# Shift and scale of the first norm: from four column quarters on VectorE to two column halves on TensorE

## The chip, the cores and the metric

The kernel runs on one core of a Trainium2 chip. The metric is device time in microseconds (us) of one execution. The engines are TensorE (PE in the profile; its weight loads are PEld), VectorE (DVE), ScalarE (ACT), GpSimd (POOL) and SyncE (SP), which here does nothing but start transfers from HBM.

## What is computed

One layer of a hybrid streaming encoder on 256 tokens of width 1024: a normalised and modulated input, a projection into two groups of heads, an output projection, and then a mixture of 32 experts, each token going to four. The change touches only the first line of the modulation:

```
c_act = silu(c)
mod = c_act @ w_ada + b_ada                      # 1024 x 6144 weights
sh1, sc1, g1, sh2, sc2, g2 = split(mod, 6)
h = rms_norm(x, pre_mix_norm) * (1.0 + sc1) + sh1
proj = h @ w_in                                  # 1024 x 2216 weights
```

The first 2048 columns of `w_ada` (8 MB in float32) give `sh1` and `sc1`. The expert weights, 384 MB, are read in full.

## The kernel before

All weights pass through a ring of seven buffers of 1 MB (`Stream`, L72, `RING` = 7). `want` lists a load, `take` gives the buffer to its user, and `done` frees it, whereupon `pump` issues the next load of the list on the SP queue. Two more buffers, `x0` and `x1`, belong to the experts; nothing uses them earlier, so the loads of two `gu` tiles into them may be issued at any time. The program is written in a logical order, and a planner that simulates the engines' times fixes the order of the instructions on each engine (`issue_after` and `keep_in_program_order` only bind it). Engines then run their own list strictly in that order.

Opening stage. `x` is normalised, scaled and transposed into `hT`, eight blocks (`k`) of 128 columns of x by 256 tokens. The matmul of the projection needs each block multiplied by `a1` = (1 + sc1) * gain and shifted by `sh1`; it is formed twice, as a rounded part `hTh` (ScalarE, L468) and a remainder `hTl` (VectorE, L470 and L471). The blocks are used in four steps `q` of two blocks each:

- `mod_sum(q)` (L444) takes two buffers `mod` holding all 1024 rows of a quarter of the columns, 256 of the shift and 256 of the scale, and adds eight products row block by row block on VectorE (L451, L453) into `md`. One row of a transfer is a contiguous run of 256 columns, 1 KB.
- `mod_use(q)` (L457) sums `md` over the partitions with four small matmuls against ones into `mc` (L459; the trace counts each as two records), adds the bias (`half`, L463), forms `a1` (L465), and then `hTh` and `hTl` of two blocks.
- `split_xbc(q)` and `split_nat(q)` cut a buffer of `w_in` into a rounded part `whi` on ScalarE (L424) and a remainder `wlo` (L427), on VectorE for xbc, on GpSimd for nat.
- `in_xbc(q)` (L483) is 48 matmuls of 256 columns into the four banks `pa`; `in_nat(q)` (L497) is 24 matmuls into the banks `pn0`, `pn1` and `pn2`. Of each three (L432, L433, L434) one needs `wlo` and one `hTl`.

After the last `in_nat` the banks `pn` are copied out (L532, L533), `gate_in` (L559) projects `z` into the banks `pz`, with its remainders on GpSimd (L563), and a long stage of attention, state-space mixing and routing follows. From about 215 us on the experts run: `up` (L1191) multiplies by `gu` tiles and `down` by `dn` tiles, all loaded through the ring.

PSUM has eight banks: four of tag A (`pa`), two of tag B (`pn0`, `pn1`) and two of tag Z, handed out in turn. Z goes to `mc`, `pn2`, then `pz0` and `pz1`: `pz0` follows `mc` and `pz1` follows `pn2`. Later (L633) the same kernel forms other columns of `mod` on TensorE: `ada` multiplies a row block by `crep`, 32 equal columns of silu(c), into four groups of 32 PSUM rows (L642).

Of the kernel before, what the change touches and what calls it, by code (L numbers as in the profile page):

```python
# [15 lines left out]
OP = mybir.AluOpType  # L16
# [4 lines left out]
S = 256  # L21
P = 128
TT = S // P
KT = D // P
# [42 lines left out]
E_C, E_PM, E_B1, E_END = 0, 8, 16, 32  # L67
# [39 lines left out]
def body(ctx, tc, a, out, ne=NE):  # L107
    nc = tc.nc
    V, A, G, T, SP = nc.vector, nc.scalar, nc.gpsimd, nc.tensor, nc.sync
# [24 lines left out]
    v1, v2, v3 = (tl([P, 2048], f"v{i}", f"v{i}") for i in (1, 2, 3))  # L134
# [32 lines left out]

    st_ = Stream(sb, [f"w{j}" for j in range(RING)])
    w_ada = a["w_ada"].rearrange("l (k p) c -> p (l k) c", p=P)
    w_adq = a["w_ada"].rearrange("l (k p) (s q c) -> p (l k) s q c", p=P, q=4, c=256)  # L170
    w_in = a["w_in"].rearrange("l (k p) c -> p (l k) c", p=P)
    w_q = a["w_q_up"].rearrange("l (k p) c -> p (l k) c", p=P)
    w_kv = a["w_kv_up"].rearrange("l (k p) c -> p (l k) c", p=P)
# [5 lines left out]
    def ld(view, src):  # L179
        def f(t):  # L180
            SP.dma_start(view(t), src)

        return f

    def want_mod(q):
        for k0 in (0, 4):

            def f(t, k0=k0):
                tv = t.rearrange("p (k s c) -> p k s c", k=4, s=2)
                for s in range(2):  # L190
                    SP.dma_start(tv[:, :, s, :], w_adq[:, k0 : k0 + 4, s, q, :])

            st_.want(f"mod{q}{k0}", f)

    def halves(t):
        return t.rearrange("p (k c) -> p k c", k=2)
# [1 line left out]
    def natv(t):  # L198
        return t[:, :1360].rearrange("p (k c) -> p k c", k=2)
# [7 lines left out]
    def ld_nat(k0):  # L207


        def f(t):  # L210
            tv = natv(t)
            SP.dma_start(tv[:, :, 0:392], w_in[:, k0 : k0 + 2, 1536:1928])
            SP.dma_start(tv[:, :, 392:424], w_in[:, k0 : k0 + 2, 2184:2216])
            SP.dma_start(tv[:, :, 424:680], w_in[:, k0 : k0 + 2, 1928:2184])

        return f

    def some(n):
        for _ in range(min(n, len(small))):
            dst, src = small.pop(0)  # L220

            def f(dst=dst, src=src):
                tc.keep_in_program_order(SP.dma_start(dst, src))

            st_.side(f)

    want_mod(0)
    for q in range(4):
        st_.want(f"xbc{2 * q}", ld(halves, w_in[:, 2 * q : 2 * q + 2, 512:1536]))
        if q < 3:  # L230
            want_mod(q + 1)
        st_.want(f"nat{2 * q}", ld_nat(2 * q))
    some(8)
    for k0 in range(0, KT, 4):
        st_.want(f"z{k0}", ld(zv, w_in[:, k0 : k0 + 4, 0:512]))
# [62 lines left out]
    ones = tl([P, P], "ones")  # L298
# [30 lines left out]
    with ExitStack() as fc:  # L329
# [106 lines left out]


        a1 = tl([P, KT], "a1")
        mc = bank("mc", "Z")

        sums = {}
        last_mod = [None]

        def mod_sum(q):  # L444
            ac = two([P, 512], "md")
            for k0 in (0, 4):
                w = st_.take(f"mod{q}{k0}").rearrange("p (k n) -> p k n", k=4)
                for k in range(4):
                    c = cact[:, k0 + k : k0 + k + 1]
                    if k0 + k == 0:  # L450
                        V.tensor_scalar(ac, w[:, k, :], c, None, op0=OP.mult)  # L451
                    else:
                        V.scalar_tensor_tensor(ac, w[:, k, :], c, ac, op0=OP.mult, op1=OP.add)  # L453
                st_.done(f"mod{q}{k0}")
            sums[q] = ac

        def mod_use(q):  # L457
            for j in range(4):
                T.matmul(mc[:, 4 * q + j : 4 * q + j + 1], sums[q][:, j * P : (j + 1) * P], ones[:, 0:1], start=q + j == 0, stop=True,  # L459
                         skip_group_check=True)  # L460
            half = two([P, 2, 2], "mh")
            ksl = slice(2 * q, 2 * q + 2)
            V.tensor_tensor(half, mc[:, 4 * q : 4 * q + 4].rearrange("p (s k) -> p s k", s=2),  # L463
                            prE[:, E_B1 : E_B1 + 16].rearrange("p (s k) -> p s k", s=2)[:, :, ksl], op=OP.add)
            V.scalar_tensor_tensor(a1[:, ksl], half[:, 1, :], 1.0, prE[:, E_PM + 2 * q : E_PM + 2 * q + 2], op0=OP.add, op1=OP.mult)  # L465
            for j in range(2):
                k = 2 * q + j
                A.activation(hTh[:, k, :], hT[:, k, :], AF.Identity, bias=half[:, 0, j : j + 1], scale=a1[:, k : k + 1])  # L468
                tm = v2[:, 1024 + S * j : 1024 + S * j + S]
                V.tensor_scalar(tm, hT[:, k, :], a1[:, k : k + 1], half[:, 0, j : j + 1], op0=OP.mult, op1=OP.add)  # L470
                last_mod[0] = V.tensor_tensor(hTl[:, k, :], tm, hTh[:, k, :], op=OP.subtract)  # L471

# [5 lines left out]
        def split_xbc(q):  # L478
            w = [halves(v) for v in split(st_.take(f"xbc{2 * q}"), wh[q % 2], wl[q % 2], parts=2)]
            st_.done(f"xbc{2 * q}")  # L480
            return w

        def in_xbc(q, w):  # L483
            k0 = 2 * q
            for k in (0, 1):
                for ct in range(8):
                    mm3(pa[ct // 2][:, ct % 2, :], [v[:, k, ct * P : (ct + 1) * P] for v in w], (hTh[:, k0 + k, :], hTl[:, k0 + k, :]),
                        k0 + k == 0 and ct % 2 == 0, k0 + k == KT - 1, skip_group_check=True)

        pn = []  # L490

        def split_nat(q):
            w = [natv(v) for v in split(st_.take(f"nat{2 * q}"), "f7", "f8", 1360, eng=G)]
            st_.done(f"nat{2 * q}")
            return w

        def in_nat(q, w):  # L497
            k0 = 2 * q
            for k in (0, 1):
                for t in range(TT):  # L500
                    h = [v[:, k0 + k, t * P : (t + 1) * P] for v in (hTh, hTl)]
                    mm3(pn[t][:, :424], h, [v[:, k, 0:424] for v in w], k0 + k == 0, k0 + k == KT - 1)
                    mm3(pn[2][:, t * 256 : t * 256 + 256], h, [v[:, k, 424:680] for v in w], k0 + k + t == 0, k0 + k == KT - 1,
                        skip_group_check=True)

        mod_sum(0)
        mod_use(0)
        pa += [bank(f"pa{j}").rearrange("p (c s) -> p c s", c=2) for j in range(4)]
        pn += [bank("pn0", "B"), bank("pn1", "B"), bank("pn2", "Z")]
        for q in range(4):  # L510
            if q == 0:
                with tc.issue_after(last_mod[0].ins):
                    wx = split_xbc(q)
            else:
                wx = split_xbc(q)
            if q < 3:
                mod_sum(q + 1)
            wn = split_nat(q)
            in_xbc(q, wx)
            if q < 3:  # L520
                mod_use(q + 1)
            in_nat(q, wn)


# [896 lines left out]
    for e in range(ne):  # L1421
# [43 lines left out]
        ac = act(e, gs, 2 if e == last else 1)  # L1465
# [40 lines left out]
    for i, tag in ((0, "gu"), (1, "pc"), (2, "tp")):  # L1506
        c0, w = parts[i]
# [65 lines left out]
```

## Time and profile before

| | us |
|---|---|
| median of three runs | 1167.58 |
| lowest and highest | 1167.48, 1169.38 |
| the profiled execution | 1165.31 |
| its span, first to last instruction | 1163.5 |
| TensorE busy in the span | 1064.9 |
| VectorE busy | 446.1 |

The profile is of one execution. A row of its timeline gives the start of a group of equal instructions, its duration, the engine, the line, what is written from what, the number of instructions, and in brackets the idle time of that engine just before and what ended it. Consecutive matmuls overlap, so the step from one start to the next is the price of one in a stream, and its duration is the latency of one. A table by stretches gives the busy time of each engine, the granted clock of TensorE (1.00 is 2.4 GHz, 0.50 is 1.2 GHz), the busy share of the transfer engines and their rate in GB/s. Some 449 MB are moved.

### The profile page before, as it was taken

How to read it: one execution, taken by the hardware profiler on the slowest of the kernel's cores; microseconds unless marked ns; L12 is line 12 of the kernel's file. 1: busy time of each engine (PE TensorE's matmuls, PEld its weight loads, DVE VectorE, ACT ScalarE, POOL GpSimd, SP SyncE). 2: the span in 40 equal slices, each digit the busy share in tenths (PEclk: the TensorE clock that was granted, in tenths of full speed). 3: DMA queues.
4: the chain of work that ended last, by engine and by line, in shares of the span. 5: the costliest groups of instructions: out<-in, count | busy, mean ns of one | idle time of the engine just before them, and what ended most of it. 6: DMA issues, size and time to landing. Idle time of an engine off the chain costs nothing. (4 is left out here: it accounts for less than half of the span.)

```text
span 1163.5 us, 13379 instructions
## 1 busy us (share of the span) xinstructions
PE 1064.9 (92%) x5078; PEld 452.4 (39%) x5078; DVE 446.1 (38%) x921; ACT 190.5 (16%) x364; POOL 68.1 (6%) x68
## 2 busy tenths in 40 slices
PE   4899998989999999998989899989898998989996
PEld 4885774333333333332323233323233232333332
DVE  6869855333332323232323232332314142323224
ACT  5365443100111100100101000100101010101003
POOL 1254430000000000000000000000000000000000
PEclk9899999999999999999999899999999898999998
DMA  9987799879989999999999999999999999999992
GB/s 337 324 328 314 262 376 361 343 290 368 412 358 422 420 406 420 421 422 420 421 420 422 420 421 420 420 421 422 419 422 422 421 422 420 421 415 420 422 356 88
DMA packets 79915, 449.23 MB, mean 386 GB/s; under 512 B 10385, under 2 KB 23166, under 8 KB 29090
## 3 DMA queue, kind: packets, MB, share of 16 engines
q1 hardware_dynamic: 79362, 447.43, 94.5%
q8 instruction: 74, 1.21, 0.4%
q14 instruction: 63, 0.52, 0.1%
q10 hardware_dynamic: 416, 0.07, 0.0%
HBM read 446.42 MB, written 1.05 MB: 385 GB/s over the span
## 5 line engine op out<-in xcount | busy, mean ns | idle before, releaser
L1195 PE MATMUL gu<-gu,xT 128*64 128x512 f32 x2048 | 475.3, 612 | 35.6 <-DMA gu<-in_w_gate_up 33.8
L1195 PEld LDWEIGHTS gu<-gu,xT 128*64 128x64 f32 x2048 | 145.5, 140 | 317.7 <-issue 262.4
L1243 PE MATMUL py<-dn,ac 128*64 128x512 f32 x992 | 220.6, 597 | 0.2 <-DVE ac L1231 0.2
L1243 PEld LDWEIGHTS py<-dn,ac 128*64 128x64 f32 x992 | 70.8, 138 | 144.6 <-issue 126.2
L1252 DVE COPY cm<-py 64x512 f32<-64x512 f32 x30 | 20.8, 695 | 212.9 <-ACT cm L1251 212.9
L1201 DVE COPY gs<-gu 128x512 f32<-128x512 f32 x31 | 21.4, 691 | 174.9 <-PE gu L1195 174.9
L1281 PE MATMUL pc<-cm,gtm 128*128 128x512 f32 x120 | 60.8, 635 | 11.5 <-DVEq L1360 10.1
L1200 ACT COPY gs<-gu 128x512 f32<-128x512 f32 x32 | 18.7, 585 | 314.0 <-PE gu L1195 314.0
L1174 PE MATMUL pg<-x,oh 128*64 128x512 f32 x256 | 60.6, 594 | 2.9 <-DVEq L1360 2.2
L1282 DVE TENSOR_TENSOR acc<-acc,pc 128x512 f32<-128x512 f32 x64 | 44.0, 687 | 39.7 <-PE pc L1281 39.6
L1536 POOL TENSOR_TENSOR x<-x,acc 128x512 f32<-128x512 f32 x1 | 1.3, 1262 | 923.8 <-ACT acc L1535 923.8
L1184 DVE TENSOR_TENSOR xT<-pgt,md 128x512 f32<-128x512 f32 x32 | 22.1, 691 | 82.8 <-PE pgt L1182 82.8
L1222 DVE TENSOR_TENSOR u<-tp,biasT 128x512 f32<-128x512 f32 x64 | 41.5, 685 | 29.4 <-PE tp L1215 29.1
L1251 ACT COPY cm<-py 64x512 f32<-64x512 f32 x30 | 17.4, 579 | 191.3 <-PE py L1243 191.3
L1170 DVE TENSOR_SCALAR oh<-cst,rkp,r 128x64 f32<-128x64 f32 x64 | 17.2, 311 | 82.0 <-PE pg L1174 82.0
L1215 PEld LDWEIGHTS tp<-ident,gs 128*128 128x128 f32 x256 | 34.6, 206 | 27.9 <-ACTq L1360 16.4
L1215 PE MATMUL tp<-ident,gs 128*128 128x128 f32 x256 | 38.0, 289 | 6.6 <-PEq L1360 5.3
L1281 PEld LDWEIGHTS pc<-cm,gtm 128*128 128x128 f32 x120 | 19.9, 193 | 52.0 <-DVEq L1360 19.8
L1176 ACT COPY xg<-pg 128x512 f32<-128x512 f32 x32 | 18.7, 585 | 127.2 <-PE pg L1174 127.2
L1228 ACT ACTIVATE sg<-u 128x512 f32<-128x512 f32 (+1 forms) x33 | 20.4, 618 | 95.5 <-DVE u L1227 91.9
L1174 PEld LDWEIGHTS pg<-x,oh 128*64 128x64 f32 x256 | 18.0, 137 | 39.4 <-issue 38.6
L1259 DVE TENSOR_SCALAR go<-cst,rkp,gate 128x64 f32<-128x64 f32 x128 | 30.0, 308 | 0.6 <-DVEq L1360 0.6
(403 smaller groups left out, 956.4 us busy)
## 6 DMA issues: line engine op xcount, KB each, us to landing
gu<-in_w_gate_up SPq DMA_DIRECT2D x256, 1024.0 KB
dn<-in_w_down SPq DMA_DIRECT2D x124, 1024.0 KB
ada<-in_w_ada SPq DMA_DIRECT2D x16, 1024.0 KB
mod<-in_w_ada SPq DMA_DIRECT2D x16, 512.0 KB
xbc<-in_w_in SPq DMA_DIRECT2D x4, 1024.0 KB
wo<-in_w_out SPq DMA_DIRECT2D x4, 1024.0 KB
z<-in_w_in SPq DMA_DIRECT2D x2, 1024.0 KB
dn<-in_w_down SPq DMA_DIRECT2D x4, 512.0 KB
```

The source lines that it names most:

```text
L1174: T.matmul(pg[64 * h : 64 * h + 64, :], oh[:, t, :], x[:, t, h * 512 : h * 512 + 512], start=t == 0, stop=t == TT - 1)
L1184: V.tensor_tensor(xT.rearrange("p (h q) s -> p q h s", h=2), pg, a2.rearrange("p (h q) -> p q h", h=2)[:, :, :, None].to_broadcast([P, 4, ...
L1195: T.matmul(gu[h][64 * g : 64 * g + 64, :], xT[:, k, :], ws[k][:, g * 1024 + h * 512 : g * 1024 + h * 512 + 512], start=k == 0, stop=k == K ...
L1201: copy(gs[1], gu[1])
L1215: T.transpose(tp[f // 4][:, f % 4].rearrange("p g s -> p (g s)"), gs[f // 4][:, rows_of(f % 4)], ident)
L1222: V.tensor_tensor(u[:, hs], tp[h], bv[:, hs, :, None].to_broadcast([P, 4, 2, CAP]), op=OP.add)
L1228: A.activation(sg[:, fs], u[:, fs, 0, :], AF.Sigmoid, scale=1.702)
L1243: T.matmul(py[64 * g : 64 * g + 64, :], ac[:, f, :], wd(f, ch), start=f == 0, stop=f == FT - 1)
L1252: V.tensor_copy(comb[(e & 1) ^ 1][64:128, :], py[64:128, :])
L1259: V.tensor_scalar(go[:, t, j, :], iota, rkp[:, t, ee : ee + 1], gate[:, t, ee : ee + 1], op0=OP.is_equal, op1=OP.mult)
L1281: T.matmul(pc, lhs(t, ch), rhs(ch), start=bias is None or (t, ch) != bias_left[0], stop=True)
L1282: V.tensor_tensor(acc[:, t, ch * 512 : ch * 512 + 512], acc[:, t, ch * 512 : ch * 512 + 512], pc, op=OP.add)
```

## The change

The columns are taken in two halves instead of four quarters, and the sum over the rows is done by TensorE. A buffer `mod` now holds two row blocks of half the columns (512 of the shift, 512 of the scale; runs of 2 KB), so a half takes four buffers. `mod_sum(h)` multiplies each row block by `crep`, in 16 matmuls that write four groups of 32 rows of one bank `mo` (row blocks even and odd, shift and scale), and copies the bank to `md` on ScalarE. `mod_use(h)` sums the groups with four small matmuls against a two-column selector `sel` into `mc`, which now lies in unused columns of the bank of `pn0`, and forms four blocks of `hTh` and `hTl`. The first half stands ahead of everything; the second is placed in step `q` = 1, between `in_xbc(1)` and `in_nat(1)`. The list of loads changes accordingly.

```
-    want_mod(0)
+    want_mod(0, (0, 2, 4, 6))
     for q in range(4):
         st_.want(f"xbc{2 * q}", ld(halves, w_in[:, 2 * q : 2 * q + 2, 512:1536]))
-        if q < 3:
-            want_mod(q + 1)
+        if q < 2:
+            want_mod(1, (4 * q,))
         st_.want(f"nat{2 * q}", ld_nat(2 * q))
+        if q < 2:
+            want_mod(1, (4 * q + 2,))
...
-        mc = bank("mc", "Z")
+        sel = tl([P, 2], "sel")
+        V.memset(sel, 0.0)
+        for g in range(4):
+            V.memset(sel[32 * g : 32 * g + 1, g % 2 : g % 2 + 1], 1.0)
+        pn = [bank("pn0", "B")]
+        mc = pn[0][:, 440:456]
...
-        def mod_sum(q):
-            ac = two([P, 512], "md")
-            for k0 in (0, 4):
-                w = st_.take(f"mod{q}{k0}").rearrange("p (k n) -> p k n", k=4)
-                for k in range(4):
-                    c = cact[:, k0 + k : k0 + k + 1]
-                    if k0 + k == 0:
-                        V.tensor_scalar(ac, w[:, k, :], c, None, op0=OP.mult)
-                    else:
-                        V.scalar_tensor_tensor(ac, w[:, k, :], c, ac, op0=OP.mult, op1=OP.add)
-                st_.done(f"mod{q}{k0}")
-            sums[q] = ac
+        def mod_sum(h):
+            b = bank("mo", "Z")
+            for k0 in range(0, KT, 2):
+                w = st_.take(f"mod{h}{k0}").rearrange("p (k s c) -> p k s c", k=2, s=2)
+                for k in range(2):
+                    for s in range(2):
+                        o = 64 * k + 32 * s
+                        T.matmul(b[o : o + 32, :], crep[:, k0 + k, :], w[:, k, s, :], start=k0 == 0, stop=k0 == KT - 2)
+                st_.done(f"mod{h}{k0}")
+            sums[h] = two([P, 512], "md")
+            A.copy(sums[h], b)
...
-            for j in range(2):
-                k = 2 * q + j
+            for j in range(4):
+                k = 4 * h + j
                 A.activation(hTh[:, k, :], hT[:, k, :], AF.Identity, bias=half[:, 0, j : j + 1], scale=a1[:, k : k + 1])
...
-            if q < 3:
-                mod_sum(q + 1)
             wn = split_nat(q)
             in_xbc(q, wx)
-            if q < 3:
-                mod_use(q + 1)
+            if q == 1:
+                mod_sum(1)
+                mod_use(1)
             in_nat(q, wn)
```

## Rows read from the trace of the kernel before

**Rows 1.** Stretches: PE, PEld, DVE, ACT, POOL busy (count), clock, DMA share, GB/s

```profile
80.00:90.00 10.00, 8.82 (x37) 5.96 (x36) 10.00 (x32) 8.26 (x15) 4.97 (x20) 1.00 0.47 166
...
230.00:240.00 10.00, 9.16 (x67) 3.44 (x67) 2.82 (x10) 1.54 (x3) 0.42 (x1) 1.00 0.02 5
...
400.00:1100.00 700.00, 648.35 (x2888) 229.39 (x2886) 217.31 (x420) 63.80 (x108) 0.00 (x0) 0.97 1.01 420
```

**Rows 2.** Waits of PE from 345 to 1130 us: total, times, longest

```profile
PE gu L1195 <- DMA gu<-in_w_gate_up: 33.8, 13, 4.6
```

**Rows 3.** Timeline of PE, opening stage: start, duration, instruction, idle before

```profile
16.44 1.87 PE L459 MATMUL mc<-ones,md 128*128 128x1 f32 x8 [1.00 <-DVE md L453]
19.46 1.22 PE L432 MATMUL pa<-hTh,whi 128*128 128x256 f32 x4 [1.15 <-ACT hTh L468]
...
27.52 0.66 PE L432 MATMUL pn<-whi,hTh 128*128 128x424 f32 x3
31.23 1.86 PE L459 MATMUL mc<-ones,md 128*128 128x1 f32 x8 [3.05 <-DVE md L453]
32.96 0.70 PE L433 MATMUL pn<-wlo,hTh 128*128 128x424 f32 x1
...
38.43 0.63 PE L432 MATMUL pa<-hTh,whi 128*128 128x256 f32 x4
...
44.07 0.67 PE L432 MATMUL pn<-whi,hTh 128*128 128x424 f32 x3
44.58 0.95 PE L459 MATMUL mc<-ones,md 128*128 128x1 f32 x8
45.39 0.44 PE L433 MATMUL pn<-wlo,hTh 128*128 128x424 f32 x1
...
48.70 0.63 PE L432 MATMUL pa<-hTh,whi 128*128 128x256 f32 x4
...
57.41 1.14 PE L459 MATMUL mc<-ones,md 128*128 128x1 f32 x8 [2.13 <-DVE md L453]
58.41 0.70 PE L433 MATMUL pn<-wlo,hTh 128*128 128x424 f32 x1
...
63.18 0.64 PE L432 MATMUL pa<-hTh,whi 128*128 128x256 f32 x4
```

**Rows 4.** Timeline of PE where the stage ends

```profile
72.67 0.28 PE L434 MATMUL pn<-whi,hTl 128*128 128x256 f32 x1
...
73.74 0.50 PE L432 MATMUL pz<-zt,hTh 128*128 128x512 f32 x1 [0.21 <-ACT qkn L533]
```

**Rows 5.** Timeline of DVE, opening stage

```profile
13.27 3.11 DVE L453 SCALAR_TENSOR_TENSOR md<-mod,cact,md 128x512 f32<-128x512 f32 x4 [0.16 <-DMA mod<-in_w_ada]
...
18.35 0.16 DVE L463 TENSOR_TENSOR mh<-mc,prE 128x4 f32<-128x4 f32 x1 [1.96 <-PE mc L459]
...
22.80 8.38 DVE L453 SCALAR_TENSOR_TENSOR md<-mod,cact,md 128x512 f32<-128x512 f32 x7
...
74.98 2.43 DVE L581 TENSOR_TENSOR ro__792<-dtk,sin 128x16 f32<-128x16 f32 x1
```

**Rows 6.** Timeline of POOL, opening stage

```profile
25.13 3.13 POOL L427 TENSOR_TENSOR wlo<-nat,whi 128x1360 fp32r<-128x1360 f32 x1 [24.69 <-ACT whi L424]
...
67.92 9.47 POOL L563 TENSOR_TENSOR zt<-z,zt 128x1024 fp32r<-128x1024 f32 x4
```

**Rows 7.** Timeline of ACT, opening stage

```profile
13.55 2.50 ACT L350 COPY hT<-tr 128x512 f32<-128x512 f32 x4 [0.99 <-PE tr L360]
...
26.18 2.00 ACT L424 CAST whi<-xbc 128x1024 fp32r<-128x1024 f32 x2 [1.13 <-DMA xbc<-in_w_in]
```

**Rows 8.** Timeline of the SP queue

```profile
18.12 1.49 SPq L181 DMA_DIRECT2D gu<-in_w_gate_up x2
```

**Rows 9.** Short stretches, columns as in the first group

```profile
32.00:34.00 2.00, 2.00 (x9) 1.95 (x9) 1.18 (x3) 0.00 (x0) 0.00 (x0) 0.50 1.10 348
...
60.00:62.00 2.00, 2.00 (x9) 1.92 (x9) 1.43 (x4) 1.02 (x2) 0.00 (x0) 0.59 1.05 405
```

**Rows 10.** Timeline of PE where `ada` runs

```profile
110.00 1.92 PE L642 MATMUL mm<-ada,v 128*32 128x512 f32 x16
```

More of the change, by code (lines that the diff above doesn't have):

```diff
@@ L169, in body @@
     w_ada = a["w_ada"].rearrange("l (k p) c -> p (l k) c", p=P)
-    w_adq = a["w_ada"].rearrange("l (k p) (s q c) -> p (l k) s q c", p=P, q=4, c=256)
+    w_adh = a["w_ada"].rearrange("l (k p) (s h c) -> p (l k) s h c", p=P, h=2, c=512)
     w_in = a["w_in"].rearrange("l (k p) c -> p (l k) c", p=P)
@@ L183, in ld, with want_mod @@
         return f
-    def want_mod(q):
-        for k0 in (0, 4):
+    def want_mod(h, ks):
+        for k0 in ks:
             def f(t, k0=k0):
-                tv = t.rearrange("p (k s c) -> p k s c", k=4, s=2)
+                tv = t.rearrange("p (k s c) -> p k s c", k=2, s=2)
                 for s in range(2):
-                    SP.dma_start(tv[:, :, s, :], w_adq[:, k0 : k0 + 4, s, q, :])
-            st_.want(f"mod{q}{k0}", f)
+                    SP.dma_start(tv[:, :, s, :], w_adh[:, k0 : k0 + 2, s, h, :])
+            st_.want(f"mod{h}{k0}", f)
     def halves(t):
@@ L438, in body @@
         a1 = tl([P, KT], "a1")
-        mc = bank("mc", "Z")
-        sums = {}
-        last_mod = [None]
-        def mod_sum(q):
-            ac = two([P, 512], "md")
-            for k0 in (0, 4):
-                w = st_.take(f"mod{q}{k0}").rearrange("p (k n) -> p k n", k=4)
-                for k in range(4):
-                    c = cact[:, k0 + k : k0 + k + 1]
-                    if k0 + k == 0:
-                        V.tensor_scalar(ac, w[:, k, :], c, None, op0=OP.mult)
-                    else:
-                        V.scalar_tensor_tensor(ac, w[:, k, :], c, ac, op0=OP.mult, op1=OP.add)
-                st_.done(f"mod{q}{k0}")
-            sums[q] = ac
@@ L457, in mod_use @@
-        def mod_use(q):
+        sel = tl([P, 2], "sel")
[4 more added lines that the diff above has]
+        mc = pn[0][:, 440:456]
+        last_mod = [None]
+        sums = {}
+        def mod_sum(h):
[9 more added lines that the diff above has]
+            A.copy(sums[h], b)
@@ L458, in mod_use @@
+        def mod_use(h):
             for j in range(4):
-                T.matmul(mc[:, 4 * q + j : 4 * q + j + 1], sums[q][:, j * P : (j + 1) * P], ones[:, 0:1], start=q + j == 0, stop=True,
+                T.matmul(mc[:, 8 * h + 2 * j : 8 * h + 2 * j + 2], sums[h][:, j * P : (j + 1) * P], sel, start=h + j == 0, stop=True,
                          skip_group_check=True)
-            half = two([P, 2, 2], "mh")
-            ksl = slice(2 * q, 2 * q + 2)
-            V.tensor_tensor(half, mc[:, 4 * q : 4 * q + 4].rearrange("p (s k) -> p s k", s=2),
+            half = two([P, 2, 4], "mh")
+            ksl = slice(4 * h, 4 * h + 4)
+            V.tensor_tensor(half, mc[:, 8 * h : 8 * h + 8].rearrange("p (k s) -> p s k", s=2),
@@ L464, in mod_use @@
                             prE[:, E_B1 : E_B1 + 16].rearrange("p (s k) -> p s k", s=2)[:, :, ksl], op=OP.add)
-            V.scalar_tensor_tensor(a1[:, ksl], half[:, 1, :], 1.0, prE[:, E_PM + 2 * q : E_PM + 2 * q + 2], op0=OP.add, op1=OP.mult)
-            for j in range(2):
-                k = 2 * q + j
+            V.scalar_tensor_tensor(a1[:, ksl], half[:, 1, :], 1.0, prE[:, E_PM + 4 * h : E_PM + 4 * h + 4], op0=OP.add, op1=OP.mult)
+            for j in range(4):
+                k = 4 * h + j
@@ L468, in mod_use @@
                 A.activation(hTh[:, k, :], hT[:, k, :], AF.Identity, bias=half[:, 0, j : j + 1], scale=a1[:, k : k + 1])
-                tm = v2[:, 1024 + S * j : 1024 + S * j + S]
+                tm = v2[:, 1024 + S * (j % 2) : 1024 + S * (j % 2) + S]
                 V.tensor_scalar(tm, hT[:, k, :], a1[:, k : k + 1], half[:, 0, j : j + 1], op0=OP.mult, op1=OP.add)
@@ L488, in in_xbc @@
                         k0 + k == 0 and ct % 2 == 0, k0 + k == KT - 1, skip_group_check=True)
-        pn = []
         def split_nat(q):
@@ L501, in in_nat @@
                     h = [v[:, k0 + k, t * P : (t + 1) * P] for v in (hTh, hTl)]
-                    mm3(pn[t][:, :424], h, [v[:, k, 0:424] for v in w], k0 + k == 0, k0 + k == KT - 1)
+                    mm3(pn[t][:, :424], h, [v[:, k, 0:424] for v in w], k0 + k == 0 and t == 1, k0 + k == KT - 1, skip_group_check=True)
                     mm3(pn[2][:, t * 256 : t * 256 + 256], h, [v[:, k, 424:680] for v in w], k0 + k + t == 0, k0 + k == KT - 1,
@@ L508, in body @@
         pa += [bank(f"pa{j}").rearrange("p (c s) -> p c s", c=2) for j in range(4)]
-        pn += [bank("pn0", "B"), bank("pn1", "B"), bank("pn2", "Z")]
+        pn += [bank("pn1", "B"), bank("pn2", "Z")]
         for q in range(4):
```

## The prediction

> **What bounds the kernel now.** I began at the end and went back. From 400 to 1100 us the transfer engines are busy without a gap, share 1.01 at 420 GB/s [rows 1], and in that part PE waits 33.8 us for `gu` tiles [rows 2]: there the end of the kernel hangs on when the transfers start to run without a stop. They do not run so earlier. From 230 to 240 us their share is 0.02 [rows 1], because all buffers are full and wait for the first expert to use them. So the start of the experts, which hangs on computing, decides when the long transfer resumes, and a microsecond won ahead of that point is a microsecond won at the end. In between, VectorE is busy 10.00 of 10 us from 80 to 90 us while the transfer share is 0.47 [rows 1]; that stage starts from the banks `pn` and is a chain of computing as well. What counts is then when the opening stage ends: its last matmul starts at 72.67 us [rows 4]. I price the change there and carry the difference to the end.
>
> In the opening stage PE starts the projection at 19.46 us, and two things stretch it [rows 3]. It waits for VectorE's sums before `mc` 3.05 us at 31.23 and 2.13 us at 57.41. After each wait the clock is down: from 32 to 34 us it is 0.50, from 60 to 62 us 0.59 [rows 9]. VectorE was late since seven additions took 8.38 us from 22.80 [rows 5], while GpSimd ran a remainder of 3.13 us from 25.13 [rows 6].
>
> **The change part by part.**
>
> *The start is later.* Before, the second `mod` buffer is what VectorE waits for up to 13.27 us [rows 5], after some 2.1 MB of `mod`. Now 4.2 MB must arrive first. Runs of 1 KB move at 348 GB/s, a stretch with `z`, in 2 KB runs, at 405 [rows 9]; no row shows `mod` itself in 2 KB runs, so these two bound it, and I take 400, since the run length is that of `z`. The second 2.1 MB then cost 5.3 us and the first 0.8 us less: the fourth buffer lands at 13.1 + 5.3 - 0.8 = 17.6 us (19.1 at 348). Behind it come the last four matmuls. In `ada`, the same shape, 16 records take 1.74 us to the next group [rows 10], so eight take 0.9 us, 1.7 at half clock, which I take because the matmuls at 16.44 ran at half the pace of those at 44.58 (1.87 against 0.95 us for eight, [rows 3]). Then the copy of the bank, 0.6 us [rows 7], and the four small matmuls, 1.9 us. `half` would start at 22.3 us instead of 18.35 [rows 5], with 0.5 us of handing over. The first projection matmul follows as before 1.1 us later, at 23.4: **+4.0 us** (+3 to +5.5). The tile of xbc arrives 1.05 MB behind the last `mod` buffer, at about 20.2 us, so its cast of 2 us [rows 7] does not delay this.
>
> *The waits go.* VectorE's 32 additions vanish, so both waits go: **-5.2 us**. With them go the half-clock stretches behind them. The 21 matmuls from 32.96 to 38.43 take 5.5 us, those from 58.41 to 63.18 4.8 us, and `in_nat(1)` takes 44.07 to 48.70, less 0.8 for `mc`, 3.8 us for 24, or 3.3 for 21 [rows 3]: 2.2 and 1.5 us, **-3.7 us**.
>
> *Small matmuls.* Three groups for `mc` stand in the projection, 1.7, 0.8 and 1.0 us to the next start [rows 3]; one of 0.8 stays: **-2.7 us**.
>
> *PE does the second sum.* 16 matmuls, 32 records at 0.109 us [rows 10]: **+3.5 us**. They lie on the path, as PE is the engine that sets the pace from 23 us on; at best those of the first two buffers fill a gap that PE has anyway.
>
> *New waits.* The trace has the two `gu` loads of 2.1 MB issued at 18.12 us, into the queue ahead of the third quarter [rows 8]. I expect them again where SP has issued its first seven tiles and waits for a buffer. Then, at 420 GB/s, nat0 lands near 25, `gu` near 30, mod12 33, xbc2 35, mod14 38, nat2 39.5, mod16 42, xbc4 45, nat4 47 and xbc6 49.5 us. PE would reach: `in_xbc(0)` to 31.5 (8.1 us, as from 19.46 to 27.52, [rows 3]), `in_nat(0)` to 35.2, `in_xbc(1)` from 36.5, since the cast of xbc2 takes 1 us for its first half. That gap is filled by the matmuls of mod10 and mod12. mod16 lands when `in_xbc(1)` ends at 42, so the second `mod_use` is covered by the 3.8 us of `in_nat(1)`: copy 0.6, small matmuls 0.8, `half` and `hTh` about 1.1. **+1.0 us** for what does not fit (0 to 3).
>
> *Two places of PSUM.* `mc` moves into the bank of `pn0`, so VectorE's read of `half` and PE's writes of `pn0` are in one bank; before, `pn` matmuls at 32.96 us follow `mc` at once [rows 3]. What this costs no row shows; it is at least nothing and at most the time to `half`, some 1 us once, and it is inside the +1.0 above. The Trainium skill, "PSUM — Partial Sum Buffer", section "PSUM bank collisions raise a hardware error", says to keep engines apart by bank and quadrant, not by address; it speaks against putting a read of `half` beside running `pn0` matmuls. By that rule half of `in_nat(1)` would wait for `half`, about 1 us; without it nothing. No row here shows either.
> The other place: `pz0` now follows `pn2`, not `mc`, in its bank. Today PE waits for the copies of `pn2` only with `pz1`, at 73.74 us [rows 4]; now the first `gate_in` matmul waits too: **+0.7 us** (0 to 1).
>
> *GpSimd.* Its four remainders of `z` run from 67.92 to 77.39 us [rows 6], 4.6 us past the end of the stage, and a 16-column operation of VectorE beside them takes 2.43 us [rows 5]. With `z` loaded earlier the first of the four can go ahead of the last nat remainder. I count half of one remainder, **-1.2 us** (0 to -2.4).
>
> *Edits with one answer.* The selector's memsets are a few VectorE operations at the start, where it idles: nothing. The transfers are fewer descriptors for the same bytes. The four blocks of `hTh` and `hTl` at once put the remainder of xbc0 about 1.5 us later on VectorE; 32 of the 48 matmuls do not need it, and at half clock they cover it.
>
> Sum: +4.0 - 5.2 - 3.7 - 2.7 + 3.5 + 1.0 + 0.7 - 1.2 = **-3.6 us**. The profiled execution would go from 1165.3 (span 1163.5 and 1.8 around it) to 1161.7. The median of the runs is 2.3 us above it, so I set the forecast against the median: 1167.6 - 3.6 = 1164.0 us.
>
> **The rivals.**
>
> *The planner's order gives the gain back (no change).* PE runs a list that was fixed by simulated times, and the wait at 31.23 us shows how it misses: `mc` was placed three matmuls into `in_nat(0)` and its data came 3 us later [rows 3]. If xbc2 or the second `mod_use` is met 1.5 to 3 us late in the same way, or the stages behind are ordered a little worse, the -3.6 becomes -2 to +1.5: 1165.5 to 1169, middle 1167.
>
> *PE waits for the second half (slower).* If the list has all of the second sum ahead of `in_xbc(1)`, PE stands from 35.2 plus 2.6 us of its first 24 records to the landing of mod16 at 42: 4.2 us, and then some 2 us at half clock, as behind the wait at 31.23. Put in place of the +1.0, that 6.2 turns -3.6 into +1.6; if the `gu` loads or xbc4 come ahead of mod16 too, another 2.6 us make it +4.2. 1169 to 1172, middle 1171. It decides against the change once mod16 is waited for longer than about 2.6 us (4.6 us of gain less 2 of slow clock). For it: the wait at 31.23. Against: mod16 stands behind xbc2 in the queue, and program order puts the sum behind `in_xbc(1)`.
>
> *PE is warm from the start (a larger gain).* PE now has matmuls between 9 and 18 us besides the transposes. If the clock is up at 23 us, `in_xbc(0)` takes the 5.7 us of `in_xbc(1)` (38.43 to 44.07, [rows 3]) instead of 8.1, and the last sums 1.7 us less: up to -4 more. Middle 1161.
>
> *Run length does not matter.* If 2 KB runs move no faster than 1 KB, the start is 1.5 us later: -2.1, 1165.5. The Trainium skill, "DMA: Bandwidth & Descriptors", section "Specifications", gives 512 B as the least for full rate and so would have it this way; the 348 against 405 GB/s [rows 9] speak against it.
>
> **How the numbers follow.** Forecast 0.43, no change 0.25, slower 0.15, larger gain 0.12, run length 0.05. This kernel can be told from no change at about 0.2%, 2.3 us. The forecast's own spread is some 1.5 us, so a fifth of it falls within 0.2%. Faster: 0.43 x 0.8 + 0.12 + 0.03 + 0.03 = 0.52; same: 0.09 + 0.21 + 0.02 = 0.32; slower: 0.15 + 0.01 = 0.16. The range reaches from the larger gain, 1160.5, to the low part of the slower case, 1170.
>
> **What would show it.** In the profile after: the first `pa` matmul near 23.4 us; no wait of PE on VectorE's `md`; the clock at 1.00 from about 28 us to the end of the stage; the 32 records of the second sum in about 3.5 us; the last `pn` matmul near 70 us and the first `pz` behind the copies of `pn2`; the near-empty stretch of transfers at 230 us some 3 to 4 us earlier; and the same rate of 420 GB/s behind it. I am wrong if PE shows a wait of over 3 us on `mod` or xbc2 after 31 us, if the stage ends at 72 us or later, or if it ends earlier and the experts do not start earlier.

## The result, and the profile after

| | before | after |
|---|---|---|
| median of five runs, us | 1167.48 | 1173.98 |
| lowest and highest | 1164.24, 1169.38 | 1171.26, 1174.57 |
| the profiled execution, us | 1165.31 | 1174.57 |
| its span | 1163.5 | 1172.8 |
| start of the last `pn` matmul of the opening stage | 72.67 | 83.02 |
| end of GpSimd's last remainder of `z` | 77.39 | 85.83 |
| start of the last group of `pk` | 99.97 | 108.69 |
| first `gu` matmul | 190.2 | 200.9 |

The ratio is 1.0051 (95% interval 1.003 to 1.0072): slower by half a per cent, outside my range of 1160.5 to 1170. By the medians the loss is 6.5 us; the two profiled executions are 9.3 us apart. In the profiles all of it is there when the opening stage ends, 10.35 us late, and the first `gu` matmul is 10.7 us late. From there on the kernel is nearly as it was: the rate of 420 GB/s is unchanged (421), the waits for `gu` are 37.0 us instead of 33.8 [rows 1, 2], and the stretch with idle transfers, from 230 to 240 us before, now lies from 240 to 250 us.

Stretches of after, columns as in [rows 1]:

```profile
48.00:50.00 2.00, 2.00 (x17) 1.98 (x15) 0.75 (x1) 2.00 (x3) 0.00 (x0) 1.00 0.04 13
...
70.00:76.00 6.00, 2.91 (x13) 2.91 (x14) 4.17 (x3) 0.00 (x0) 1.88 (x1) 0.50 0.50 165
...
240.00:250.00 10.00, 9.18 (x62) 3.37 (x63) 2.82 (x10) 1.54 (x3) 0.42 (x1) 1.00 0.04 16
```

The timeline of PE in after, columns as in [rows 3]; it answers to [rows 3, 4]:

```profile
18.57 1.06 PE L457 MATMUL mo<-mod,v 128*32 128x512 f32 x6 [0.30 <-DMA mod<-in_w_ada]
...
24.95 0.58 PE L434 MATMUL pa<-hTh,whi 128*128 128x256 f32 x1 [3.57 <-ACT whi L426]
...
32.91 1.92 PE L457 MATMUL mo<-mod,v 128*32 128x512 f32 x16
...
39.16 1.05 PE L457 MATMUL mo<-mod,v 128*32 128x512 f32 x2
...
45.06 1.06 PE L457 MATMUL mo<-mod,v 128*32 128x512 f32 x6
...
46.55 1.06 PE L457 MATMUL mo<-mod,v 128*32 128x512 f32 x8
...
52.62 0.74 PE L434 MATMUL pa<-hTh,whi 128*128 128x256 f32 x4 [0.41 <-ACT hTh L473]
...
59.60 0.49 PE L434 MATMUL pz<-zt,hTh 128*128 128x512 f32 x1 [0.56 <-ACT zt L564]
...
60.78 0.46 PE L435 MATMUL pn<-wlo,hTh 128*128 128x424 f32 x1 [0.69 <-POOL wlo L429]
...
66.63 0.39 PE L434 MATMUL pa<-hTh,whi 128*128 128x256 f32 x1 [1.87 <-ACT whi L426]
...
73.09 0.58 PE L436 MATMUL pa<-hTh,wlo 128*128 128x256 f32 x1 [5.24 <-DVE wlo L429]
...
83.02 0.28 PE L436 MATMUL pn<-whi,hTl 128*128 128x256 f32 x1
...
84.09 0.51 PE L434 MATMUL pz<-zt,hTh 128*128 128x512 f32 x1 [0.72 <-ACT qkn L535]
```

Both waits for `md` are gone, as I had it, and up to 59 us PE hardly waits. Then come four waits, the longest 5.24 us for a remainder of the last tile of xbc. From 70 to 76 us the clock is 0.50, so the matmuls behind that wait run at half pace too. What VectorE did meanwhile stands in its own timeline and GpSimd's:

```profile
69.00 2.91 DVE L675 COPY ev<-hd 128x8 f32<-128x8 f32 x1 [14.01 <-DMA hd<-in_a_log]
71.82 2.35 DVE L429 TENSOR_TENSOR wlo<-xbc,whi 128x1024 fp32r<-128x1024 f32 x2
```

```profile
68.83 3.05 POOL L429 TENSOR_TENSOR wlo<-nat,whi 128x1360 fp32r<-128x1360 f32 x1 [3.41 <-ACT whi L426]
81.09 4.74 POOL L565 TENSOR_TENSOR zt<-z,zt 128x1024 fp32r<-128x1024 f32 x2 [9.21 <-ACT zt L564]
```

VectorE was idle for 14.01 us ahead of a copy of 8 columns. It copies `hd`, a small table that nothing else reads before 85 us, and its transfer landed at 69.0. The remainder that PE waited for stood behind it on VectorE's list. The copy then took 2.91 us beside a remainder on GpSimd, against 0.16 us in e11 without one (the last section has more), so more than half of what the remainder lost came after the landing. In before the same copy waits the same way, but behind the last remainder, where it holds up nothing; no row of mine ahead of the prediction shows it. VectorE's timeline of before:

```profile
57.27 2.35 DVE L427 TENSOR_TENSOR wlo<-xbc,whi 128x1024 fp32r<-128x1024 f32 x2
...
69.73 0.61 DVE L673 COPY ev<-hd 128x8 f32<-128x8 f32 x1 [8.25 <-DMA hd<-in_a_log]
```

The planner puts the copy by simulated times, and in after it came out ahead.

The tile itself was late as well. The SP queue of after first issues small tables, from 40.89 to 48.33 us, then `nat` for step 2 behind a load of `z`, and `xbc` for step 3 behind two of `z` and two of `wq`:

```profile
49.15 0.39 SPq L181 DMA_DIRECT2D z<-in_w_in  x1
49.64 0.45 SPq L212 DMA_DIRECT2D nat<-in_w_in  x1
...
51.43 0.42 SPq L181 DMA_DIRECT2D z<-in_w_in  x1
51.94 0.47 SPq L181 DMA_DIRECT2D wq<-in_w_q_up  x1
52.47 0.51 SPq L223 DMA_DIRECT2D v<-in_w_q_up  x1
53.07 0.42 SPq L181 DMA_DIRECT2D xbc<-in_w_in  x1
```

ScalarE then waits for that last tile:

```profile
65.54 2.00 ACT L426 CAST whi<-xbc 128x1024 fp32r<-128x1024 f32 x2 [5.02 <-DMA xbc<-in_w_in]
```

In before SP issues the last `xbc` at 44.67 us, ahead of the tables and of the first `z` (55.79). SP's waits between the tables of after, the longest 2.2 us up to 46.56, end with earlier transfers, and the one of 0.5 us ahead of `z` too; none of them ends with the second sum on PE. Meanwhile the transfers stand (13 GB/s from 48 to 50 us).

### The profile page after: what moved, and what is told of

Its sections match the earlier page's. It is cut to its first block, busy times and chain, and to the rows that moved or that the text cites. A ratio compares the mean times of both kernels' runs of the same rounds, so it can differ in the third digit from the quotient of the medians.

```text
span 1172.8 us, 13441 instructions
## 1 busy us (share of the span) xinstructions
PE 1068.4 (91%) x5123; PEld 450.1 (38%) x5126; DVE 417.9 (36%) x890; ACT 191.2 (16%) x366; POOL 65.9 (6%) x68
```

## The experiments

Theory after this reading: (1) the place of the copy on VectorE makes the loss; (2) the order of the loads makes a smaller part; (3) the change itself, with both out of the way, brings what I forecast. Rivals: the loads make it all, and the copy only fills VectorE's idle time; or the sums on TensorE cost more than they save. A fourth idea, that GpSimd and not PE ends the opening stage, came out of the first eight runs, and the last four test it. All kernels compute the full output.

Table: median of 5 to 12 runs, ratio to before with its 95% interval, and, from the profile, starts in us of the last `pn` matmul (PE), the end of GpSimd's remainders of `z` (Gp), the last group of `pk`, and the first `gu` matmul. The kernel before had medians of 1166.77, 1165.64 and 1165.93 in the three groups of runs (e1, e2, e5, e6; e7 to e10; e11 to e14).

| run | median | ratio | PE | Gp | pk | gu |
|---|---|---|---|---|---|---|
| before | | 1 | 72.67 | 77.39 | 99.97 | 190.2 |
| after | 1173.98 | 1.0051 [1.003, 1.0072] | 83.02 | 85.83 | 108.69 | 200.9 |
| e1_hd_copy_last | 1167.64 | 1.0008 [0.9994, 1.0023] | 76.71 | 79.52 | 102.38 | 192.7 |
| e2_load_order | 1165.65 | 0.9993 [0.9981, 1.0004] | 74.27 | 78.02 | 100.69 | 190.8 |
| e6_before_hd_copy_first | 1176.24 | 1.0072 [1.0056, 1.0088] | 72.83 | 90.92 | 111.22 | 201.8 |
| e8_loads_only | 1175.69 | 1.008 [1.006, 1.01] | 83.24 | 86.05 | 108.90 | 202.2 |
| e10_late_start_alone | 1172.34 | 1.0072 [1.0045, 1.0099] | 76.00 | 82.18 | 104.79 | 195.1 |
| e5_quarters_on_pe | 1171.94 | 1.0039 [1.0025, 1.0053] | 71.37 | 76.12 | 100.05 | 195.6 |
| e9_quarters_all_orders | 1167.70 | 1.0023 [1.001, 1.0037] | 70.67 | 76.28 | 100.35 | 192.5 |
| e7_all_orders | 1165.86 | 0.9998 [0.9987, 1.0009] | 72.27 | 78.40 | 101.10 | 191.5 |
| e11_z_on_vector | 1163.32 | 0.9973 [0.9962, 0.9984] | 72.14 | none | 97.81 | 191.3 |
| e12_before_z_on_vector | 1166.14 | 1.0001 [0.9987, 1.0016] | 73.31 | none | 98.93 | 189.4 |
| e13_quarters_z_on_vector | 1165.94 | 0.9992 [0.9979, 1.0004] | 73.95 | none | 99.68 | 191.4 |
| e14_e2_z_on_vector | 1163.76 | 0.998 [0.9968, 0.9993] | 72.66 | none | 98.32 | 188.6 |

**The copy alone.** In after, the copy is kept behind everything that stands ahead of it in the program; the loads stay as the planner has them.

```
-        V.tensor_copy(av, hd[:, 1, :])
+        tc.keep_in_program_order(V.tensor_copy(av, hd[:, 1, :]))
```

> The changed kernel, with the 8-column copy from hd on VectorE put behind the last remainder of xbc in VectorE's list; nothing else is altered, the order of the transfers stays. Theory (two orders share the loss, and this one keeps the last remainder waiting from 67 to 72 us): the remainder starts when the cast is there, at about 66.6 us, the 5.2 us wait of PE before it goes to about 1, no half-clock stretch at 70 to 76 us; the last pn matmul starts near 77 us instead of 83.02, and the time falls by some 5 to 6 us, to about 1168.5. Rival (the loss is the later start and the second sum on TensorE, the wait only fills time that would be lost anyway): within 1.5 us of 1174.

The ratio falls from 1.0051 to 1.0008 and the stage ends at 76.71, near the 77 that I expected. The remainder now runs at once (VectorE's timeline of e1); PE's wait of 5.24 us and the half clock behind it are gone, a wait of 1.77 us for the late tile stays:

```profile
66.95 2.36 DVE L429 TENSOR_TENSOR wlo<-xbc,whi 128x1024 fp32r<-128x1024 f32 x2 [12.15 <-ACT whi L426]
```

**The loads.** In after, the loads of xbc, nat and z are pinned in the order of the list (`keep_in_program_order` around each `dma_start`). Planned anew, the copy fell behind the last remainder of itself; e8 is the same with the copy put ahead again by `issue_after`.

> The changed kernel, with the loads of xbc, nat and z kept in the order of the list on the SP queue: nat4 and xbc6 are no longer issued behind z and the second nat tile. In this kernel the planner then also puts the copy from hd behind the last remainder. Theory (loads in the wrong order): nat4 lands near 46 us instead of 56, xbc6 near 50 instead of 65.5; no wait of PE over 1 us between 53 us and the end of the stage; the last pn matmul starts near 72 us, the time is 1166 to 1168, about that of the kernel before. Rival (the start at 25 us and the second sum hold the stage up by themselves): the last pn matmul not before 77 us, 1171 or more.

> The changed kernel with the loads of xbc, nat and z in list order, but the copy from hd kept ahead of the last remainder on VectorE, where the changed kernel has it. With the two earlier runs it makes a table of two by two. Theory (the copy alone decides, since hd lands at about 70 us whatever the loads of xbc do): the last remainder runs from 70 to 72.4 us although xbc6 is there at 56, PE waits for it some 6 us, last pn matmul at 79 to 81 us, the time 1171 to 1173. Rival (the late loads were the cause and the copy only rode on them): last pn matmul near 74 us, 1165 to 1167.

Together with after and e1 this is a table of two by two. Copy ahead: 1.0051 with planned loads, 1.008 with pinned ones. Copy behind: 1.0008 and 0.9993. The copy's place is worth 0.4 to 0.9%. The order of the loads makes no difference in time that can be told: with the copy behind it is 0.15% faster, with it ahead 0.3% slower, and both times the intervals overlap; the stage ends 2.4 us earlier with it (74.27 against 76.71) when the copy is behind. VectorE in e8:

```profile
70.89 0.75 DVE L525 COPY ev<-hd 128x8 f32<-128x8 f32 x1 [10.73 <-DMA hd<-in_a_log]
71.55 4.53 DVE L435 TENSOR_TENSOR wlo<-xbc,whi 128x1024 fp32r<-128x1024 f32 x2
```

The loads were in order, and the stage ended as late as in after (83.24, where I expected 79 to 81, and 1175.69 us against 1171 to 1173). So the rival "the loads make it all" falls. The size is a miss: PE's list was planned anew, it waits 2.94 us for the remainder and 3.4 us in three waits ahead of it, and the remainder took 4.53 us beside GpSimd instead of 2.36. In e2 the stage ends at 74.27 us, not near 72, and another order shows: GpSimd's list has a remainder of `z` ahead of the last of `nat`, and PE waits 1.73 us for the latter at 71.03 us.

**The copy alone, in before.**

```
+            elif q == 3:
+                ahead = V.tensor_copy(eva[:, TT, :], hd[:, 1, :])
+                with tc.issue_after(ahead.ins):
+                    wx = split_xbc(q)
```

> The kernel before, with only the 8-column copy from hd put ahead of the last remainder of xbc in VectorE's list, as the changed kernel has it. Theory (this order alone is worth some 5 us): hd lands at about 69.5 us, the last remainder runs from then to 72 instead of from 57.27 us, PE waits about 4 us in the last in_xbc and is at half clock behind it; last pn matmul near 79 us instead of 72.67, the time 1172 to 1174. Rival: within 1.5 us of 1167.5.

The old kernel with this copy put ahead is 0.72% slower (1176.24 us, where I expected 1172 to 1174). VectorE and PE of e6, one row each:

```profile
69.53 6.79 DVE L427 TENSOR_TENSOR wlo<-xbc,whi 128x1024 fp32r<-128x1024 f32 x2
```

```profile
84.85 0.70 PE L432 MATMUL pz<-zt,hTh 128*128 128x512 f32 x1 [3.90 <-ACT zt L567]
```

The wait that I expected in the last `in_xbc` is not there. The planner also moved the last `in_nat` ahead of `in_xbc`, so the loss lies not ahead of the last `pn` matmul (72.83, not near 79) but behind it, in `gate_in`: PE waits 3.90 and 1.98 us there for the parts of `z`, and from 85 to 89 us the clock is 0.50. So the orders alone, without any part of the change, can cost the old kernel as much as the change lost; that it is the same wait, this run does not show.

**Parts of the change.** e5 keeps four quarters of 1 KB runs and sums them on TensorE with the selector, loads pinned and the copy last; e9 pins the loads of wq and wkv and GpSimd's order too. e10 is the kernel before with the first two `mod` quarters both loaded ahead of the first tile of xbc, the second in front, all orders pinned: the late start without the sums on TensorE.

```
-    want_mod(0)
+    want_mod(1)
+    want_mod(0)
```

> The kernel before, with its four quarters and two buffers each, but each quarter summed by TensorE (16 matmuls of 256 columns into four groups of 32 rows, copied by ScalarE, added by the two-column selector), the loads of xbc, nat and z in list order, and the copy from hd behind the last remainder. It tells the halves from the change of engine. Theory (the halves cost the late start, the change of engine takes away VectorE's delays): the first pa matmul starts near 19.5 us, no waits on md; last pn matmul near 68 us, the time 1162 to 1165. Rival (TensorE sums cost what they save): 1167 to 1169.

> Four quarters summed by TensorE as in the earlier run, now with wq and wkv in list order too and GpSimd's remainders of z behind the last one of nat. That run reached the end of its opening stage early (last full pn matmul at 71.4 us) and lost 5 us between 140 and 181 us, with the clock at 0.71 from 140 to 150. Theory (that loss was the order of the later loads and of the small copies): last pn matmul near 71 us, first gu matmul near 189 us, the time 1162 to 1165. Rival (the loss behind belongs to the order that the planner finds for this kernel): again 1170 to 1172 with the first gu matmul near 195 us.

> The kernel before, summing on VectorE, with the two loads of the second quarter ahead of those of the first, so that the projection starts some 5 us later as in the changed kernel, but the second quarter is summed by then; loads of xbc, nat, z, wq and wkv in list order, the copy from hd last. Theory (PE sets the pace once it has started, and what counts is the start plus its work plus waits): first pa matmul near 24.7 us instead of 19.46, no wait at 31 us, last pn matmul at 71 to 74 us, the time within 2 us of 1166.8. Rival (a late start is lost in full): last pn matmul at 77 to 78 us, 1171 to 1172.

In e10, with VectorE still doing the sums, the first `pa` matmul starts at 26.37 us, later than in after (24.95) and than the 24.7 that I expected, the last `pn` matmul at 76.00 instead of 71 to 74, and the time is 0.72% above before, nearer to the rival. PE waits 7.17 us for VectorE's additions, and VectorE's first large operation behind them lies beside GpSimd, 3.54 us for two. PE and VectorE of e10:

```profile
22.53 1.86 PE L466 MATMUL mc<-ones,md 128*128 128x1 f32 x8 [7.17 <-DVE md L460]
```

```profile
24.89 3.54 DVE L477 TENSOR_SCALAR v<-hT,a,mh 128x256 f32<-128x256 f32 x2
```

The quarters end PE's stage 1.3 us (e5) and 2 us (e9, 70.67) ahead of before and gain no time from it. Both are misses: I expected 1162 to 1165 us, and they took 1171.94 and 1167.70. Between the two the intervals overlap; in the profiled execution of e5 the clock is 0.71 from 140 to 150 us, and why is not settled.

**All orders.** e2 with wq, wkv and GpSimd's remainders pinned as well, the copy last, and ScalarE's cast of the first tile of xbc ahead of the third and fourth block of `hTh`.

> The changed kernel with every order that the traces found wrong put right: loads of xbc, nat, z, wq and wkv in list order, the copy from hd behind the last remainder, GpSimd's remainders of z behind the last one of nat, and on ScalarE the cast of the first xbc tile ahead of blocks 2 and 3 of hTh. Theory (the change itself is worth about 1 to 3 us, the orders took 6 to 9 away): against the run with the loads in order, 1 us is won at the start (PE's 3.6 us wait for the cast becomes 2.6), 1.7 us before the last in_nat; last pn matmul near 71.5 us instead of 74.3, the time 1162 to 1164.5, faster than the kernel before by 2 to 4 us. Rival (the second sum and the late start eat the gain whatever the order): last pn matmul at 74 us or later, 1165 to 1167.

PE's stage ends at 72.27 instead of 74.27 us, and nothing is gained: 1165.86 us, where I expected 1162 to 1164.5, and `pk` starts 0.4 us later than in e2. So part (3) of the theory does not hold: with the orders mended, the -3.6 us do not come. With e9 that is twice that PE was early to no end. What did not come earlier is GpSimd. Before, e7 and e9, each with its GpSimd row and the VectorE row beside it (before's are in [rows 5, 6]); first GpSimd and VectorE of e7:

```profile
68.94 9.46 POOL L579 TENSOR_TENSOR zt<-z,zt 128x1024 fp32r<-128x1024 f32 x4
```

```profile
74.09 1.99 DVE L597 TENSOR_TENSOR ro__784<-dtk,cos 128x16 f32<-128x16 f32 x1
76.00 2.43 DVE L597 TENSOR_TENSOR ro__785<-dtk,sin 128x16 f32<-128x16 f32 x1
```

then the same of e9:

```profile
66.79 9.49 POOL L571 TENSOR_TENSOR zt<-z,zt 128x1024 fp32r<-128x1024 f32 x4
```

```profile
73.86 2.46 DVE L589 TENSOR_TENSOR ro__826<-dtk,sin 128x16 f32<-128x16 f32 x1
```

GpSimd ends at 77.39, 78.40 and 76.28 us, VectorE's operation of 16 columns at 77.41, 78.43 and 76.32. Behind it on VectorE stands the convolution `xc`, behind that on ScalarE the casts `qkT`, and PE waits for those. PE of before, then of e7:

```profile
88.91 1.98 PE L605 MATMUL pk<-wkv,qkT 128*128 128x512 f32 x4 [1.01 <-ACT qkT L553]
...
99.97 1.88 PE L605 MATMUL pk<-wkv,qkT 128*128 128x512 f32 x4
```

```profile
86.83 1.56 PE L609 MATMUL pq<-wq,qkT 128*128 128x384 f32 x4 [1.61 <-ACT qkT L569]
...
90.04 1.98 PE L621 MATMUL pk<-wkv,qkT 128*128 128x512 f32 x4 [1.01 <-ACT qkT L569]
```

In seven of the nine kernels with the remainders on GpSimd that are not e6, `pk` starts 22.58 to 22.86 us behind GpSimd's end. In e9 it is 24.07: PE ran there at 0.62 of the clock from 88 to 92 us; in e5 it is 23.93, and PE waited there 2.22 us for VectorE's copy `qkn` up to 77.20 us.

**The remainders of z on VectorE**, which is idle from 60 to 72 us: in e7 (e11), in before with the copy last (e12), in e9 (e13), and in e7 without the moved cast (e14).

```
-            G.tensor_tensor(zt[:, 1], zc, zt[:, 0], op=OP.subtract)
+            V.tensor_tensor(zt[:, 1], zc, zt[:, 0], op=OP.subtract)
```

> The kernel of e7_all_orders, with the four remainders of z on VectorE instead of GpSimd; nothing else. Theory (what ends the opening stage for the stage behind is GpSimd, not PE): in the trace of before GpSimd's remainders of z end at 77.39 us and VectorE's 16-column operation that stood beside them ends at 77.41; in e7 the two are 78.40 and 78.43, in e9 76.28 and 76.32. With the remainders on VectorE, four of 1.18 us in its idle time from 60 to 72 us, the 16-column operations take 0.16 us each from 74 us on, the convolution of xc starts near 74.5 instead of 78.7, and PE's two waits for the casts of qkT, 1.61 and 1.01 us in e7, go: last pk matmul near 99.9 instead of 102.4, first gu matmul near 189, about 2.5 us ahead of e7 and 1.2 ahead of before, time 0.2% below e7's. Rival (the gain is taken by something else of that stage, VectorE's ada additions or the tables of ScalarE): pk and gu within 0.7 us of e7, same time.

> The kernel before, with the four remainders of z on VectorE and the copy from hd behind them on its list; nothing else. Theory (GpSimd ends the stage): VectorE is free at about 74.6 instead of 77.4 us, the 16-column operation takes 0.16 us instead of 2.43; PE has only 0.17 + 1.01 us of waits for qkT to give back, so last pk matmul near 100.2 instead of 101.3 and first gu matmul near 189.0, time 0.1% lower than before. Rival (something else of that stage sets it): pk and gu within 0.4 us of before.

> The kernel of e9_quarters_all_orders (quarters summed on TensorE, all orders pinned) with the four remainders of z on VectorE; nothing else. Theory (GpSimd ends the stage): in e9 PE waited 2.01 us for qkT at 87.59 and then ran at 0.76 of the clock, pk 2.48 and pq 2.70 us instead of 1.98 and 1.45; both go. First gu matmul near 189 instead of 192.5 us, time 0.3% below e9's, level with or under before. Rival: pk and gu within 0.7 us of e9.

> The change with all loads of the opening stage in list order, the copy from hd behind the last remainder and the four remainders of z on VectorE (e11 without the moved cast of the first xbc tile). Theory (GpSimd ends the stage): the nat remainder of GpSimd is no longer behind one of z, so PE's wait of 1.73 us at 71.03 in e2 goes too; first gu matmul between that of e11 and 1 us later, as the start is up to 0.7 us later; time within 0.1% of e11. Rival: as e2, gu near 190.8.

(The expectations count to the last matmul of `pk`, 1.3 us behind the start of its group.) VectorE and PE of e11:

```profile
68.76 2.36 DVE L579 TENSOR_TENSOR zt<-z,zt 128x1024 fp32r<-128x1024 f32 x2 [4.16 <-ACT zt L578]
...
73.95 0.16 DVE L597 TENSOR_TENSOR ro__784<-dtk,cos 128x16 f32<-128x16 f32 x1
74.04 0.17 DVE L597 TENSOR_TENSOR ro__785<-dtk,sin 128x16 f32<-128x16 f32 x1
```

```profile
84.92 1.46 PE L609 MATMUL pq<-wq,qkT 128*128 128x384 f32 x4
...
97.81 1.88 PE L621 MATMUL pk<-wkv,qkT 128*128 128x512 f32 x4
```

Both waits for `qkT` are gone and `pk` starts 3.3 us earlier than in e7, as the theory had it. In all four kernels `pk` now starts 25.62 to 25.73 us behind the last `pn` matmul, whatever the kernel: PE sets the pace. The time of e11 is 0.9973 of before, 0.25% below e7's, and e14 has 0.998; these are the only kernels here that are faster than before beyond their intervals. e12, before with the same move, gains 1.0 us at `pk` and 0.8 at `gu`, but no time that can be told (1.0001). So neither half brings the gain: the change without the move has 0.9998 (e7) and 0.9993 (e2), both within their intervals of 1, the move without the change 1.0001. From e7 to e11 the intervals stand apart, from e2 to e14 they overlap. The move takes away two things at once, GpSimd's own time and VectorE's operations held beside it; PE's waits point at the second, but no run parts them.

Missed: `gu` in e11, expected near 189, is at 191.3; in that profiled execution the clock is 0.66 from 140 to 150 us, and it took 1165.07 us, 1.75 above its median. e14 has 1.00 before and behind, and 188.6. And `gu` in e13 is 2.4 us behind what I expected, since its list was planned anew and PE's stage ended 3.3 us later than in e9.

## Why the prediction was wrong, point by point

*What bounds the kernel.* That a loss at the end of the opening stage reaches the end is borne out by the profiles: 10.35 us at the last `pn` matmul, 10.7 at the first `gu`, 9.3 in the span; the medians are 6.5 us apart. That a gain does is not: "what counts is then when the opening stage ends: its last matmul" took PE alone. The stage behind begins when the later of two is done, PE (plus 25.65 us to `pk`) and GpSimd's remainders of `z` (plus 22.6); both numbers are read from these same kernels. For before that gives 98.3 and 99.99 us; it measured 99.97 us, so GpSimd was the later one by 1.7. The later of the two gives the start of `pk` within 0.1 us in 11 of the 14 kernels of the table; e5 and e9 are 1.3 and 1.5 us later than that, and in e6 `gate_in` itself waited. I had both rows [rows 5, 6], read the stuck operation, and then entered GpSimd as a credit of -1.2 us in a sum of PE's path. It was the other path, and there a gain of PE is worth nothing unless GpSimd's end moves too.

*What cost the time.* This is the step that failed: the sum took VectorE's last remainder to be in time and put the order on its list at nothing. It has no term for it, and the rival "the planner's order gives the gain back" priced such a slip at 1.5 to 3 us, on the data of the second sum. It happened on a small table: an order that put one instruction with a late transfer in front of a remainder on which PE waits. Its price followed from rows that I could have had: the landing of `hd` near 69 us, against a last `in_xbc` that starts at 63.18 [rows 3], plus the half clock behind a wait of that length [rows 9]. That the copy would be held by GpSimd until 71.91 us comes on top. Of 6.3 us that e1 gives back at the stage's end, 5.24 are the wait; the rest fits the slow matmuls behind it. The rival "PE waits for the second half" did not come: the 16 matmuls stand in four pieces, none with a wait for `mod`.

*The terms.* They can be read in e14, where the three orders are out of the way and the last `pn` matmul starts at 72.66 us, just as before. I had near 70, so 3.1 us are missing:

```profile
18.58 1.06 PE L463 MATMUL mo<-mod,v 128*32 128x512 f32 x6 [0.31 <-DMA mod<-in_w_ada]
...
24.95 0.58 PE L440 MATMUL pa<-hTh,whi 128*128 128x256 f32 x1 [3.56 <-ACT whi L432]
...
52.88 0.75 PE L440 MATMUL pa<-hTh,whi 128*128 128x256 f32 x4 [0.41 <-ACT hTh L479]
...
72.66 0.28 PE L442 MATMUL pn<-whi,hTl 128*128 128x256 f32 x1
```

- *The start*: +5.5 us, not +4.0. The fourth buffer landed at 18.57 us instead of 17.6, yet `half` starts at 21.42 us in after, 0.9 ahead of the 22.3 that I had: the clock was 0.94 from 20 to 22 us (1.00 in e14), so the small matmuls did not run at half pace. The rival "PE is warm from the start" came true that far. The miss is behind `half`: 3.5 us to the first `pa` matmul instead of 1.1, and by then the clock was 0.50. ScalarE did all four blocks of `hTh` (2.08 us, to 23.9) ahead of the cast that the first matmul needs. I had that cast as covered because its tile lands early; what it needed was ScalarE. ScalarE in after:

```profile
21.88 2.08 ACT L473 ACTIVATE hTh<-hT,mh,a 128x256 fp32r<-128x256 f32 x4 [1.61 <-DVE a L470]
23.87 1.97 ACT L426 CAST whi<-xbc 128x1024 fp32r<-128x1024 f32 x2
```

- *The second sum*: 4.8 us, not 3.5. The list cuts it into four pieces of 16, 2, 6 and 8 records, which are all 32; from the start of each to the next group it is 1.85, 0.98, 0.99 and 1.00 us in after. A piece of two records cost as much as one of eight, so my price of 0.109 us a record, from one stream of 16, does not carry over: the pieces of two and six, by their count one buffer's, cost 1.97 us together instead of 0.87. The trace of before has a short piece of this form too, 1.00 us to the next group, which I did not use:

```profile
107.91 1.06 PE L642 MATMUL mm<-ada,v 128*32 128x512 f32 x8
108.91 1.16 PE L757 MATMUL at<-kT,qT 98*128 98x128 f32 x8
```

- *Right*: both waits for `md` gone (-5.2); the clock 1.00 from 30 us on in e14, so no half-clock stretches (-3.7); one small group in place of three; `pz` 0.72 us behind the copies of `pn2` (+0.7); both `gu` loads issued at 21.11 us ahead of the second tile of xbc, and no wait from it. *New waits* were 0.41 us, not 1.0.
- *The bank shared by `mc` and `pn0`*: no wait of PE stands there in after or e14, so what I weighed there cost nothing that shows.
- *Run length*: the rival that it does not matter falls. While the first half lands in runs of 2 KB, from 8 to 18 us, after moves 396 GB/s; before moves 359 from 6 to 12 us, in runs of 1 KB.

The late start (1.55) and the longer second sum (1.3) make 2.9 us of the missing 3.1; the new waits give back 0.6, and 0.8 stays unaccounted for. Put through the rule of the two ends, even my own -3.1 at PE would have brought nothing to `pk` as long as GpSimd's end stays. The chance of "slower" (0.16) was on another mechanism; no change, which I gave 0.25 as a rival, is what the change is worth with its orders mended.

*What stays open.* By the profiles, e14 is 1.6 us ahead of before at `gu` and e11 1.1 behind, with the clock of that one stretch; the medians say 2.2 and 2.6 us ahead. Profiled before took 1165.31 us, 2.2 below its median. How often the low clock from 140 to 150 us comes in each kernel, single profiles can't tell.

## What to carry to other kernels

When a planner or a hand-made list fixes each engine's order, a change moves instructions that it does not touch: list every instruction on the late path's engines whose input is a transfer, however small, and price what stands behind it if it comes first. Before you carry a gain to the end, ask which engine really ends the stage; where two of them do, a gain on one is worth only what the other lets through, and an engine that is "4.6 us past the end" may be the end. When a change that should pay brings nothing, mend the order first and look for the second end then: here the change and the move of `z` were each worth nothing that can be told, and together 0.2 to 0.3%.

## What the runs showed of the hardware

An operation of VectorE that takes two tensors from SBUF, issued while GpSimd runs a TENSOR_TENSOR, was held until that GpSimd instruction ended, and only then took its own time; most often the next one was then held by the next. In e7 GpSimd's four instructions from 68.94 us, 2.365 us each, end at 76.04 and 78.40 (the last two); VectorE's two operations of 16 columns end at 76.08 and 78.43, 1.99 and 2.43 us instead of 0.16. In e10 one operation of 0.16 us passes in between, at 79.74 us, and the one behind it takes 2.38. Two remainders of 1024 columns took 4.44 us in e7 from 56.11 us, beside a GpSimd instruction that ends at 58.33, against 2.36 us alone. The copy from `hd`, one tensor from SBUF, met it too: 69.00 to 71.91 us in after, beside a GpSimd remainder that ends at 71.88, against 0.16 us in e11; so did the TENSOR_SCALAR of e10 above. Copies from PSUM at the same time did not: `qkn` from `pn` took 0.56 us in before (73.06 us) beside GpSimd and 0.56 in e11 without.

The Trainium skill, "GPSIMD Engine Reference", section "1. Specifications", says that the SBUF interfaces are shared with VectorE and contended by operations with two SBUF inputs or in a mode that uses two ports. The runs agree for the operations with two inputs from SBUF; whether the copy and the TENSOR_SCALAR, with one, ran in such a mode no run shows. The price in these runs is the rest of the GpSimd instruction, up to 2.4 us for a remainder of `z`.
